# A row-wise log-sum-exp on one core: scalar-engine results in PSUM, more rows for VectorE, logs moved early, a new chunk plan

## The chip, the cores and the metric

One core of a Trainium2 chip. The time is device microseconds of one execution. Every run told here was with a granted clock of 1.0. Five engines run side by side; three matter here. The load queue moves the input from HBM to SBUF, ScalarE (ACT in the profile) computes exponentials and logarithms, and VectorE (DVE) adds up rows. PSUM is the second on-chip memory; in these kernels ScalarE writes results to it and ScalarE and VectorE read them from there.

## The reference

```python
x = np.random.randn(32, 512, 1024).astype(np.float32)
x_max = np.max(x, axis=-1, keepdims=True)
return x_max.squeeze(-1) + np.log(np.sum(np.exp(x - x_max), axis=-1))
```

These are 16,384 rows of 1024 numbers, 128 rows on each of 128 partitions. Both kernels leave the maximum out and compute log(sum(exp(x))).

## The kernel before

The kernel loads the 128 rows of each partition in chunks that become smaller. In a pair such as `(16, 9)`, the first number is the rows of the chunk. The second is how many of them go through ScalarE as one large exponential and are then summed by VectorE. Each of the other rows is one exponential with `accum_out`, which makes ScalarE itself add up the row. The exponentials overwrite the input; only the sums are wanted.

```python
CHUNKS = [
    (12, 4), (14, 4), (16, 4), (16, 9), (16, 11), (12, 8), (10, 6), (8, 5),
    (6, 4), (5, 3), (4, 2), (3, 1), (2, 0), (2, 0), (1, 0),
]
LAST_PARTS = [512, 512]
RING_ROWS = 50
# ... tiles in SBUF: ring [128, 50, 1024], sums [128, 128], part [128, 2], res [128, 128]
    for r, n_dve in CHUNKS:
        # ... slot of the ring
        nc.sync.dma_start(out=ring[:, slot : slot + r], in_=x_v[:, row : row + r])
        if n_dve:
            nc.scalar.activation(out=ring[:, slot : slot + n_dve],
                                 in_=ring[:, slot : slot + n_dve], func=Exp)
            nc.vector.reduce_sum(out=sums[:, row : row + n_dve],
                                 in_=ring[:, slot : slot + n_dve], axis=AX)
        for j in range(n_dve, r):
            nc.scalar.activation(out=ring[:, slot + j], in_=ring[:, slot + j], func=Exp,
                                 accum_out=sums[:, row + j : row + j + 1])
        # ...
    # last row: two loads of 512 columns, each with an accumulating Exp into part[:, k];
    # after the first of them: Ln of all 127 finished rows
    nc.vector.reduce_sum(out=sums[:, row : row + 1], in_=part, axis=AX)
    nc.scalar.activation(out=res[:, row : row + 1], in_=sums[:, row : row + 1], func=Ln)
    nc.scalar.dma_start(out=out_v, in_=res)
```

The softmax here doesn't subtract the row's maximum and nothing guards it: scores larger than these inputs give would overflow.

## Time and profile before

| | before |
|---|---|
| median of the first 3 runs | 166.25 us (166.19 to 166.28) |
| span of the profiled run | 164.9 us |
| last load byte arrives | 159.09 us |
| last half row started on ScalarE | 161.31 us |
| output issued | 162.48 us |

The last load byte comes from the trace's records of single DMA packets; the rows below it are ScalarE's own start times. All are counted from the start of the span.

First the page of before: span, busy time of the engines, the busy tenths of the DMA engines in 40 slices of 4.1 us, and the load queue (packets, MB, share of the time of 16 DMA engines).

```profile
span 164.9 us, 255 instructions
...
DVE 67.1 (41%) x13; ACT 125.7 (76%) x151; POOL 0.2 (0%) x4
...
DMA  6998999997997998999899898999999999999940
...
q1 hardware_dynamic: 2448, 67.11, 95.3%
```

The load queue is busy for 95.3% of the span. The packet records run from 1.74 us to 159.09 us, which is 67.11 MB at 427 GB/s. In the DMA line only the first slice and the last two are low. So about 157 us of the 165 is one unbroken load, and no change of arithmetic shortens it. What can be shortened is the end, after the last byte.

The groups of instructions by form show what one accumulating row costs (busy us, mean ns of one).

```profile
L67 ACT ACTIVATE ring<-ring 128x1024 f32<-128x1024 f32 x66 | 68.7, 1043 | 0.0
...
L67 ACT ACTIVATION_READ_ACCUMULATOR ring<-ring 128x1 f32 x66 | 12.5, 190 | 0.0
```

One row is two instructions, an ACTIVATE of 1043 ns and an ACTIVATION_READ_ACCUMULATOR of 190 ns. They overlap their neighbours, so their sum is not the cost of a row. The cost is the distance from start to start, and that is read from the timeline of ScalarE (start us, length us, what; in brackets the idle time before it and what ended it):

```profile
130.08 4.47 ACT L60 ACTIVATE ring<-ring 128x5120 f32<-128x5120 f32 x1 [0.23 <-DMA ring<-in_x_dram]
...
143.44 2.76 ACT L60 ACTIVATE ring<-ring 128x3072 f32<-128x3072 f32 x1 [0.18 <-DMA ring<-in_x_dram]
...
148.38 1.91 ACT L60 ACTIVATE ring<-ring 128x2048 f32<-128x2048 f32 x1
...
158.42 1.05 ACT L67 ACTIVATE ring<-ring 128x1024 f32<-128x1024 f32 x1
159.36 0.20 ACT L67 ACTIVATION_READ_ACCUMULATOR ring<-ring 128x1 f32 x1
159.46 1.05 ACT L67 ACTIVATE ring<-ring 128x1024 f32<-128x1024 f32 x1
...
161.11 0.31 ACT L92 ACTIVATE res<-sums 128x127 f32<-128x127 f32 x1
161.31 0.63 ACT L84 ACTIVATE ring<-ring 128x512 f32<-128x512 f32 x1
161.82 0.20 ACT L84 ACTIVATION_READ_ACCUMULATOR ring<-ring 128x1 f32 x1
162.25 0.20 ACT L94 ACTIVATE res<-sums 128x1 f32<-128x1 f32 x1 [0.22 <-DVE sums L93]
162.48 0.37 ACTq L95 DMA_DIRECT2D out_dram<-res  x1
```

From 158.42 to 159.46 is 1.04 us: that is one row. The view puts an idle time in brackets only from 0.15 us on. The chunk at 148.38 has none, but the trace has 0.10 us of idle time before it, and its landing is where the chain that ended last (`--critical`) comes in from the loads. From 148.38 until the last Ln ScalarE does not idle, so there it is behind the loads. The last half row could have been started about 0.47 us after the last byte. This is the time at other places between the last packet of a chunk and the exponential that had waited for it: the eight-row chunk's last packet ended at 129.61, and 130.08 is the start. It was started 2.22 us after the last byte, at 161.31. VectorE's timeline at the end:

```profile
153.35 1.22 DVE L63 TENSOR_REDUCE sums<-ring 128x1 f32<-128x1024 f32 x1 [0.74 <-ACT ring L60]
162.06 0.15 DVE L93 TENSOR_REDUCE sums<-part 128x1 f32<-128x2 f32 x1 [7.48 <-ACT ring L84]
```

VectorE had nothing to do for 7.48 us, then added two numbers in 0.15 us, and ScalarE waited 0.22 us for that. From the start of the last half row to the issue of the output is 1.17 us.

### The profile page before, as it was taken

How to read it: one execution, taken by the hardware profiler on the slowest of the kernel's cores; microseconds unless marked ns; L12 is line 12 of the kernel's file. 1: busy time of each engine (PE TensorE's matmuls, PEld its weight loads, DVE VectorE, ACT ScalarE, POOL GpSimd, SP SyncE). 2: the span in 40 equal slices, each digit the busy share in tenths (PEclk: the TensorE clock that was granted, in tenths of full speed). 3: DMA queues.
4: the chain of work that ended last, by engine and by line, in shares of the span. 5: the costliest groups of instructions: out<-in, count | busy, mean ns of one | idle time of the engine just before them, and what ended most of it. 6: DMA issues, size and time to landing. Idle time of an engine off the chain costs nothing.

```text
span 164.9 us, 255 instructions
## 1 busy us (share of the span) xinstructions
DVE 67.1 (41%) x13; ACT 125.7 (76%) x151; POOL 0.2 (0%) x4
## 2 busy tenths in 40 slices
DVE  0000073005400082000099200999996949788300
ACT  3000699249990799919996299999989999999993
POOL 0000000000000000000000000000000000000000
DMA  6998999997997998999899898999999999999940
GB/s 191 477 477 382 445 445 445 445 445 318 509 461 318 493 511 366 397 509 413 350 509 461 358 453 382 421 437 477 389 437 421 427 423 432 426 411 417 415 187 16
DMA packets 2593, 67.18 MB, mean 407 GB/s; under 512 B 288, under 2 KB 416, under 8 KB 800
## 3 DMA queue, kind: packets, MB, share of 16 engines
q1 hardware_dynamic: 2448, 67.11, 95.3%
q10 hardware_dynamic: 144, 0.07, 0.1%
q14 instruction: 1, 0.01, 0.0%
HBM read 67.11 MB, written 0.07 MB: 407 GB/s over the span
## 4 chain that ended last, share of the span: by engine, by line
DMA 54%; ACT 32%; DVE 8%; another core or an unknown queue 3%; issue 1%; SPq 0%; ACTq 0%
DMA ring<-in_x_dram 54%; ACT ring L60 16%; ACT ring L67 15%; DVE sums L63 8%; ACT ring L84 1%; SPq L58 0%; ACT res L94 0%; ACT res L92 0%; DVE sums L93 0%; ACTq L60 0%; ACTq L92 0%
## 5 line engine op out<-in xcount | busy, mean ns | idle before, releaser
L63 DVE TENSOR_REDUCE sums<-ring 128x4 f32<-128x4096 f32 (+8 forms) x12 | 66.9, 5576 | 87.7 <-ACT ring L60 87.7
L60 ACT ACTIVATE ring<-ring 128x4096 f32<-128x4096 f32 (+8 forms) x12 | 54.5, 4539 | 35.8 <-DMA ring<-in_x_dram 35.7
L67 ACT ACTIVATE ring<-ring 128x1024 f32<-128x1024 f32 x66 | 68.7, 1043 | 0.0
L67 ACT ACTIVATION_READ_ACCUMULATOR ring<-ring 128x1 f32 x66 | 12.5, 190 | 0.0
L93 DVE TENSOR_REDUCE sums<-part 128x1 f32<-128x2 f32 x1 | 0.2, 155 | 7.5 <-ACT ring L84 7.5
L52 ACT ACT_TABLE_LOAD x1 | 1.3, 1283 | 0.7 <-PEq L112 0.7
L84 ACT ACTIVATE ring<-ring 128x512 f32<-128x512 f32 x2 | 1.3, 628 | 0.0
L84 ACT ACTIVATION_READ_ACCUMULATOR ring<-ring 128x1 f32 x2 | 0.4, 202 | 0.0
L94 ACT ACTIVATE res<-sums 128x1 f32<-128x1 f32 x1 | 0.2, 203 | 0.2 <-DVE sums L93 0.2
L92 ACT ACTIVATE res<-sums 128x127 f32<-128x127 f32 x1 | 0.3, 308 | 0.0
L112 POOL MEMSET const-bfloat16-1.0<- 128x1 bf16 x1 | 0.1, 102 | 0.0
L112 POOL MEMSET const-uint8-127<- 128x1 uint8 x1 | 0.1, 102 | 0.0
L112 POOL MEMSET const-float32-0.0<- 128x1 f32 x1 | 0.1, 99 | 0.2 <-issue 0.2
L112 POOL MEMSET const-float32-1.0<- 128x1 f32 x1 | 0.1, 99 | 0.0
## 6 DMA issues: line engine op xcount, KB each, us to landing
ring<-in_x_dram SPq DMA_DIRECT2D x2, 6144.0 KB, 27.4
ring<-in_x_dram SPq DMA_DIRECT2D x1, 7168.0 KB, 33.9
ring<-in_x_dram SPq DMA_DIRECT2D x1, 5120.0 KB, 28.3
ring<-in_x_dram SPq DMA_DIRECT2D x1, 4096.0 KB, 14.7
ring<-in_x_dram SPq DMA_DIRECT2D x1, 3072.0 KB, 21.6
ring<-in_x_dram SPq DMA_DIRECT2D x1, 2560.0 KB, 27.3
ring<-in_x_dram SPq DMA_DIRECT2D x1, 2048.0 KB, 24.1
ring<-in_x_dram SPq DMA_DIRECT2D x2, 1024.0 KB, 30.4
```

The lines of the kernel that those rows point to most:

```text
L52: nc.scalar.preload_act_table_set("natural_log_exp_and_others")
L60: nc.scalar.activation(out=ring[:, slot : slot + n_dve], in_=ring[:, slot : slot + n_dve], func=Exp)
L63: nc.vector.reduce_sum(out=sums[:, row : row + n_dve], in_=ring[:, slot : slot + n_dve], axis=AX)
L67: nc.scalar.activation(out=ring[:, slot + j], in_=ring[:, slot + j], func=Exp, accum_out=sums[:, row + j : row + j + 1],)
L84: nc.scalar.activation(out=ring[:, slot, c : c + w], in_=ring[:, slot, c : c + w], func=Exp, accum_out=part[:, k : k + 1],)
L92: nc.scalar.activation(out=res[:, 0:row], in_=sums[:, 0:row], func=Ln)
L93: nc.vector.reduce_sum(out=sums[:, row : row + 1], in_=part, axis=AX)
L94: nc.scalar.activation(out=res[:, row : row + 1], in_=sums[:, row : row + 1], func=Ln)
L112: nc = _bacc.Bacc("TRN2", target_bir_lowering=False, num_devices=1)
```

## The change

The intent was to make ScalarE cheaper at the end: results that nobody reads go to PSUM, and so do most accumulators; more rows of the late chunks go to VectorE; logs of finished rows are taken early; and the last two half sums are joined by Ln itself, as log(1·a + b), without VectorE.

```diff
 CHUNKS = [
-    (12, 4), (14, 4), (16, 4), (16, 9), (16, 11), (12, 8), (10, 6), (8, 5),
-    (6, 4), (5, 3), (4, 2), (3, 1), (2, 0), (2, 0), (1, 0),
+    (10, 4), (16, 6), (16, 6), (16, 10), (15, 10), (13, 8), (11, 7), (8, 5),
+    (6, 4), (5, 4), (3, 2), (3, 2), (2, 1), (1, 0), (1, 0), (1, 0),
 ]
+LN_FROM = 5
 ...
+    apool = ctx.enter_context(tc.tile_pool(name="apool", bufs=4, space=bass.MemoryType.PSUM))
+    jpool = ctx.enter_context(tc.tile_pool(name="jpool", bufs=2, space=bass.MemoryType.PSUM))
 ...
+    def exp_sum(src, w, to):
+        junk = jpool.tile([P, D], fp32, name="junk")
+        nc.scalar.activation(out=junk[:, :w], in_=src, func=Exp, accum_out=to)
 ...
-        for j in range(n_dve, r):
-            nc.scalar.activation(out=ring[:, slot + j], in_=ring[:, slot + j], func=Exp,
-                                 accum_out=sums[:, row + j : row + j + 1])
+        if r - n_dve >= 2:
+            acc = apool.tile([P, r - n_dve], fp32, name="acc")
+            for j in range(n_dve, r):
+                exp_sum(ring[:, s + j], D, acc[:, j - n_dve : j - n_dve + 1])
+            nc.vector.tensor_copy(sums[:, row0 + n_dve : row0 + r], acc)
+        elif r > n_dve:
+            exp_sum(ring[:, s + n_dve], D, sums[:, k : k + 1])
+        if r >= LN_FROM:
+            if row0 > logged:
+                nc.scalar.activation(out=res[:, logged:row0], in_=sums[:, logged:row0], func=Ln)
+                logged = row0
 ...
-    nc.vector.reduce_sum(out=sums[:, row : row + 1], in_=part, axis=AX)
-    nc.scalar.activation(out=res[:, row : row + 1], in_=sums[:, row : row + 1], func=Ln)
+    last = apool.tile([P, 1], fp32, name="acc")
+    exp_sum(ring[:, slot, w0:], w1, last)
+    nc.scalar.activation(out=res[:, row:NB], in_=last, func=Ln, bias=part)
```

(The two forms of the loop are joined over several lines here, and the index `k` is `row0 + n_dve`. The whole diff also turns on `tc.manual_schedule()`. Run e1 below is without it and e2 with it, and their stretches differ by no more than the early Ln, so no effect of it was seen.) There is one thing that the diff doesn't show and the built program does. In a chunk with two or more such rows, every exponential into `acc` except the first waits for the one just before it to complete, because both write the same PSUM tile. There are 42 such waits. In the kernel before there were no such waits: there, two columns of one SBUF tile did not make one row wait for another.

More of the change, by code (lines that the diff above doesn't have):

```diff
@@ L46 @@
     pool = ctx.enter_context(tc.tile_pool(name="pool", bufs=1))
+    apool = ctx.enter_context(tc.tile_pool(name="apool", bufs=4, space=bass.MemoryType.PSUM))
+    jpool = ctx.enter_context(tc.tile_pool(name="jpool", bufs=2, space=bass.MemoryType.PSUM))
     ring = pool.tile([P, RING_ROWS, D], fp32, name="ring")
     sums = pool.tile([P, NB], fp32, name="sums")
-    part = pool.tile([P, len(LAST_PARTS)], fp32, name="part")
+    part = pool.tile([P, 1], fp32, name="part")
     res = pool.tile([P, NB], fp32, name="res")
     nc.scalar.preload_act_table_set("natural_log_exp_and_others")
+    def exp_sum(src, w, to):
+        junk = jpool.tile([P, D], fp32, name="junk")
+        nc.scalar.activation(out=junk[:, :w], in_=src, func=Exp, accum_out=to)
+    ctx.enter_context(tc.manual_schedule())
     row = slot = 0
+    logged = 0
+    w0, w1 = LAST_PARTS
+    plan = []
     for r, n_dve in CHUNKS:
@@ L57 @@
             slot = 0
-        nc.sync.dma_start(out=ring[:, slot : slot + r], in_=x_v[:, row : row + r])
-        if n_dve:
-            nc.scalar.activation(
-                out=ring[:, slot : slot + n_dve], in_=ring[:, slot : slot + n_dve], func=Exp
-            )
-            nc.vector.reduce_sum(
-                out=sums[:, row : row + n_dve], in_=ring[:, slot : slot + n_dve], axis=AX
-            )
-        for j in range(n_dve, r):
-            nc.scalar.activation(
-                out=ring[:, slot + j],
-                in_=ring[:, slot + j],
-                func=Exp,
-                accum_out=sums[:, row + j : row + j + 1],
-            )
+        plan.append((row, slot, r, n_dve))
         slot += r
@@ L77 @@
         slot = 0
-    c = 0
-    for k, w in enumerate(LAST_PARTS):
-        nc.sync.dma_start(out=ring[:, slot, c : c + w], in_=x_v[:, row, c : c + w])
-        c += w
-    c = 0
-    for k, w in enumerate(LAST_PARTS):
-        nc.scalar.activation(
-            out=ring[:, slot, c : c + w],
-            in_=ring[:, slot, c : c + w],
-            func=Exp,
-            accum_out=part[:, k : k + 1],
-        )
-        c += w
-        if k == 0:
-            nc.scalar.activation(out=res[:, 0:row], in_=sums[:, 0:row], func=Ln)
-    nc.vector.reduce_sum(out=sums[:, row : row + 1], in_=part, axis=AX)
-    nc.scalar.activation(out=res[:, row : row + 1], in_=sums[:, row : row + 1], func=Ln)
+    for row0, s, r, n_dve in plan:
+        nc.sync.dma_start(out=ring[:, s : s + r], in_=x_v[:, row0 : row0 + r])
+        if n_dve:
+            nc.scalar.activation(
+                out=ring[:, s : s + n_dve], in_=ring[:, s : s + n_dve], func=Exp
+            )
+            nc.vector.reduce_sum(
+                out=sums[:, row0 : row0 + n_dve], in_=ring[:, s : s + n_dve], axis=AX
+            )
+        if r - n_dve >= 2:
[4 more added lines that the diff above has]
+        elif r > n_dve:
+            k = row0 + n_dve
+            exp_sum(ring[:, s + n_dve], D, sums[:, k : k + 1])
+        if r >= LN_FROM:
+            if row0 > logged:
+                nc.scalar.activation(
+                    out=res[:, logged:row0], in_=sums[:, logged:row0], func=Ln
+                )
+                logged = row0
+    nc.sync.dma_start(out=ring[:, slot, :w0], in_=x_v[:, row, :w0])
+    nc.sync.dma_start(out=ring[:, slot, w0:], in_=x_v[:, row, w0:])
+    exp_sum(ring[:, slot, :w0], w0, part)
+    nc.scalar.activation(out=res[:, logged:row], in_=sums[:, logged:row], func=Ln)
+    last = apool.tile([P, 1], fp32, name="acc")
+    exp_sum(ring[:, slot, w0:], w1, last)
+    nc.scalar.activation(out=res[:, row:NB], in_=last, func=Ln, bias=part)
     nc.scalar.dma_start(out=out_v, in_=res)
```

## The prediction

> **What bounds it now.** The page of before: span 164.9 us, ScalarE 76% busy, VectorE 41%, load queue 95.3% of the DMA engines' time, 67.11 MB read. The packet records run from 1.7 to 159.1 us without a gap: 427 GB/s. So about 157 us is loading, which the change doesn't shorten. Only the tail, 159.1 to 164.9 us, can shrink. The timeline of ScalarE shows it without a real gap from 148.4 us (landing of the four-row chunk) to the last accumulator read at 162.0; landings are seen about 0.47 us after the last packet, so the last half row could have been started at 159.6 and was started at 161.3: ScalarE has about 1.7 us of backlog. Then VectorE's join (0.16), Ln (0.20), hand-overs of 0.04, and 2.4 us of output.
>
> **Costs in the trace.** A row with accumulation repeats every 1.04 us (ACTIVATE 1043 ns plus ACTIVATION_READ_ACCUMULATOR 190 ns, each overlapping its successor by 95 ns). A row in a block costs 0.853 us plus 0.1 per block; VectorE then 1.07 per row.
>
> **What changes.**
> 1. Rows summed by VectorE 61 -> 69: 8 x 0.187 = 1.5 us less on ScalarE, mostly before the tail; in the last 22-23 rows 10 -> 13, about 0.5 us.
> 2. Ten early Ln of 6 to 16 columns, about 0.12 us each, three of them after 138 us: +0.3. The late Ln falls from 308 to about 0.2 us.
> 3. Junk and most accumulators in PSUM. The Trainium skill ("Perfetto Trace Analysis", Optimizing Scalar/DVE Operations) gives ScalarE 93 ns access overhead on SBUF, 51 on PSUM, and says that the profile shows about twice this. Our 190 ns agrees for SBUF; nothing here shows PSUM. I estimate 0 to 45 ns off each instruction, 0 to 80 ns per row.
> 4. A new wait: in the built program each accumulating exponential into a shared accumulator tile, except the first, waits for the one before to complete; its 95 ns overlap is lost and a 40 ns hand-over added. Without PSUM's saving such a row would take 1.17 us, with it about 1.05 to 1.13. Single-row chunks wait only on the row before last: no stall.
> 5. VectorE join removed (0.2 saved); Ln with a bias operand costs about 0.09 more (estimate from "ScalarE: Activation LUTs", What ACT_TABLE_LOAD costs). Net 0.1.
> 6. Smaller last loads: packet times of before (162 ns for 4 KB against 2443 for 64 KB) give +0.1 us of loading. Ring slots still come free 7 us or more before the queue runs dry.
>
> **Sum.** Following ScalarE row by row (for before this gives 161.9; measured 162.0): at 1.04/1.17 us per row it ends at 162.9, at 1.00/1.09 at 161.9, at 0.96/1.05 at 161.2. It cannot be under about 160.5. The accumulator waits hand back most of what the VectorE rows save; only cheaper PSUM writes make it a gain. I take between the last two: 165.8 us, range 164.7 to 167.1. Under 162.9 would need more than the whole backlog.
>
> **What would show it.** Last load byte at about 159.2. Read accumulator to PSUM under 190 ns; start-to-start in groups 1.05 to 1.17; single late rows 0.96 to 1.04. Last half row's start before 161.3 for a gain. VectorE's last reduction near 159, just before the late Ln. Last accumulator read to Ln: one short same-engine wait.
>
> **What would make it wrong.** PSUM writes no cheaper (up to 167) or far cheaper (164.5); the late Ln waiting for VectorE; a changed DMA rate.

## The result

| | before | after |
|---|---|---|
| median, first comparison | 166.26 us (4 runs) | 166.59 us (4 runs, 166.43 to 167.12) |
| ratio after/before, 95% interval | | 1.0025 [1.0002, 1.0048] |
| ratio in a second comparison, on another chip | | 1.0006 [0.9991, 1.0022] |
| span of the profiled run | 164.9 us | 164.9 us |
| last load byte | 159.09 us | 158.88 us |
| last half row started (behind the last byte) | 161.31 (2.22) | 161.35 (2.47) |
| output issued (after that start) | 162.48 (1.17) | 162.31 (0.96) |

A ratio is the mean time of one kernel's fast runs over that of the other's fast runs of the same rounds, so it isn't quite the ratio of the medians quoted. The change does next to nothing to the time. The two comparisons put it at 0.06% and 0.25% slower, and their intervals run from 0.09% faster to 0.48% slower. The page of after has the same shape:

```profile
span 164.9 us, 258 instructions
...
DVE 76.2 (46%) x22; ACT 126.6 (77%) x145; POOL 0.2 (0%) x4
...
DMA  6999997997997998999889999999999999999940
...
q1 hardware_dynamic: 2592, 67.11, 95.2%
```

VectorE has 9 us more work and the load queue is as full as before. The forms of one accumulating row:

```profile
L60 ACT ACTIVATE junk<-ring 128x1024 f32<-128x1024 f32 x58 | 59.3, 1022 | 1.3
...
L60 ACT ACTIVATION_READ_ACCUMULATOR junk<-ring 128x1 f32 x60 | 8.1, 135 | 0.0
```

Each of the two instructions has become shorter: 1043 to 1022 ns, and 190 to 135 ns. A reader who adds these lines up expects rows cheaper by about 75 ns. The timeline shows the opposite:

```profile
121.24 6.18 ACT L80 ACTIVATE ring<-ring 128x7168 f32<-128x7168 f32 x1 [0.70 <-DMA ring<-in_x_dram]
127.32 1.01 ACT L60 ACTIVATE junk<-ring 128x1024 f32<-128x1024 f32 x1
128.26 0.12 ACT L60 ACTIVATION_READ_ACCUMULATOR junk<-ring 128x1 f32 x1
128.42 1.03 ACT L60 ACTIVATE junk<-ring 128x1024 f32<-128x1024 f32 x1
129.38 0.13 ACT L60 ACTIVATION_READ_ACCUMULATOR junk<-ring 128x1 f32 x1
129.54 1.03 ACT L60 ACTIVATE junk<-ring 128x1024 f32<-128x1024 f32 x1
...
131.68 0.20 ACT L97 ACTIVATE res<-sums 128x13 f32<-128x13 f32 x1
131.78 4.46 ACT L80 ACTIVATE ring<-ring 128x5120 f32<-128x5120 f32 x1
...
158.55 1.01 ACT L60 ACTIVATE junk<-ring 128x1024 f32<-128x1024 f32 x1
159.50 0.19 ACT L60 ACTIVATION_READ_ACCUMULATOR junk<-ring 128x1 f32 x1
159.59 1.01 ACT L60 ACTIVATE junk<-ring 128x1024 f32<-128x1024 f32 x1
...
161.24 0.20 ACT L105 ACTIVATE res<-sums 128x16 f32<-128x16 f32 x1
161.35 0.58 ACT L60 ACTIVATE junk<-ring 128x512 f32<-128x512 f32 x1
161.87 0.12 ACT L60 ACTIVATION_READ_ACCUMULATOR junk<-ring 128x1 f32 x1
162.01 0.26 ACT L108 ACTIVATE res<-acc,part 128x1 f32<-128x1 f32 x1
162.31 0.37 ACTq L109 DMA_DIRECT2D out_dram<-res  x1
```

From 127.32 to 128.42 is 1.10 us, and to 129.54 another 1.12. In the trace's nanoseconds the read of the accumulator ends at 128.388 and the next row starts at 128.420. In before the next row started about 0.1 us *before* the read ended (159.46 against 159.36 + 0.20); now it starts 0.03 us after. The early Ln at 131.68 moves the next start by 0.10 us, to 131.78. The single rows at the end (158.55, 159.59) are 1.04 us apart as before. There is no bracket after 121.24, and the trace has no smaller gap over 0.04 us there, so ScalarE has not idled from the landing of the 11-row chunk on. VectorE in the same time:

```profile
148.85 9.93 DVE L83 TENSOR_REDUCE sums<-ring 128x4 f32<-128x4096 f32 x4 [1.24 <-ACT ring L80]
```

This is four reductions in one merged line. It ends at 158.78, well ahead of the late Ln at 161.24, so VectorE does not hold it up.

### The profile page after: what moved, and what is told of

Its sections match the earlier page's. It is cut to its first block, busy times and chain, and to the rows that moved or that the text cites. A ratio compares the mean times of both kernels' runs of the same rounds, so it can differ in the third digit from the quotient of the medians.

```text
span 164.9 us, 258 instructions
## 1 busy us (share of the span) xinstructions
DVE 76.2 (46%) x22; ACT 126.6 (77%) x145; POOL 0.2 (0%) x4
## 3 DMA queue, kind: packets, MB, share of 16 engines
q1 hardware_dynamic: 2592, 67.11, 95.2%
HBM read 67.11 MB, written 0.07 MB: 407 GB/s over the span
## 4 chain that ended last, share of the span: by engine, by line
DMA 54%; ACT 32%; DVE 11%; issue 2%; SPq 0%
DMA ring<-in_x_dram 54%; ACT ring L80 22%; DVE sums L83 11%; ACT junk L60 9%; ACT res L97 0%; SPq L78 0%; ACT res L108 0%; ACT res L105 0%
## 5 line engine op out<-in xcount | busy, mean ns | idle before, releaser
L83 DVE TENSOR_REDUCE sums<-ring 128x4 f32<-128x4096 f32 (+7 forms) x13 | 75.3, 5812 | 71.3 <-ACT ring L80 71.3
L80 ACT ACTIVATE ring<-ring 128x4096 f32<-128x4096 f32 (+7 forms) x13 | 61.4, 4726 | 33.6 <-DMA ring<-in_x_dram 33.6
L60 ACT ACTIVATE junk<-ring 128x1024 f32<-128x1024 f32 (+1 forms) x60 | 60.5, 1008 | 1.3
L60 ACT ACTIVATION_READ_ACCUMULATOR junk<-ring 128x1 f32 x60 | 8.1, 135 | 0.0
L90 DVE COPY sums<-acc 128x6 f32<-128x6 f32 (+5 forms) x9 | 1.4, 158 | 11.2 <-ACT junk L60 11.2
L97 ACT ACTIVATE res<-sums 128x16 f32<-128x16 f32 (+6 forms) x9 | 1.8, 203 | 0.0
```

The lines of the kernel that those rows point to most:

```text
L60: nc.scalar.activation(out=junk[:, :w], in_=src, func=Exp, accum_out=to)
L80: nc.scalar.activation(out=ring[:, s : s + n_dve], in_=ring[:, s : s + n_dve], func=Exp)
L83: nc.vector.reduce_sum(out=sums[:, row0 : row0 + n_dve], in_=ring[:, s : s + n_dve], axis=AX)
L90: nc.vector.tensor_copy(sums[:, row0 + n_dve : row0 + r], acc)
L97: nc.scalar.activation(out=res[:, logged:row0], in_=sums[:, logged:row0], func=Ln)
```

## A measure for the experiments

The loading differs from run to run. In the profiled runs the last byte arrived between 158.75 and 159.31 us, also for one and the same kernel (158.88 and 158.75 for the kernel after). This spread of 0.56 us is as large as most effects here. But the time after the last byte has two parts that hardly vary. The *lag* is from the last byte to the start of the last half row. It was 2.47 and 2.48 us in the two profiles of the kernel after, and 2.22 us in both profiles of kernels with before's plan and rows. The *end part* is from that start to the issue of the output. Where ScalarE no longer waits for loads after the 11-row chunk of the new plan, there is also the *stretch*: from the start of that chunk's large exponential to the start of the last half row, ScalarE's own work without idle time (only e5 has 0.06 us of it). It was 40.11 us in both profiles of the kernel after.

| run | one row to the next in a group, us | stretch, us | lag, us | end part, us | ratio to before, 95% interval |
|---|---|---|---|---|---|
| before | 1.04 | – | 2.22 | 1.17 | 1 |
| after | 1.12 | 40.11 | 2.47 | 0.96 | 1.0025 [1.0002, 1.0048] |
| after_again | 1.12 | 40.11 | 2.48 | 0.96 | 1.0006 [0.9991, 1.0022] |
| e1_plan_only | 1.04 | 39.43 | 1.84 | 1.16 | 0.9990 [0.9978, 1.0003] |
| f2_psum_junk_only | 1.04 | 39.43 | 1.84 | 1.16 | 0.9979 [0.9967, 0.9991] |
| e2_sbuf_acc | 1.04 | 39.74 | 2.13 | 0.96 | 0.9989 [0.9977, 1.0002] |
| f3_one_junk | 1.18 | 41.18 | 3.54 | 0.98 | 1.0083 [1.0069, 1.0096] |
| e3_two_acc | 1.00 | 39.36 | 1.74 | 1.00 | 0.9968 [0.9954, 0.9981] |
| e7_late_two_acc | 1.12, then 1.00 | 39.37 | 1.73 | 0.99 | 0.9966 [0.9948, 0.9983] |
| e4_no_early_ln | 1.12 | 39.81 | 2.21 | 0.96 | 0.9992 [0.9979, 1.0004] |
| e5_two_acc_few_ln | 1.00 | 39.21 | 1.55 | 0.96 | 0.9967 [0.9949, 0.9985] |
| f1_join_only | 1.04 | – | 2.22 | 0.99 | 0.9998 [0.9986, 1.0011] |
| e6_finer_plan | 1.00 | – | 1.19 | 0.97 | 0.9944 [0.9928, 0.9960] |

All of them give the reference's result. Kernels e1 to e4 ran together on one chip, e5 to e7 with after_again on another, f1 to f3 in a third call; each of these was timed in five rounds. The chips differ a little: before itself took 166.53, 166.40 and 166.38 us. The absolute times in the expectations start from the first comparison, so the ratios are what to compare.

## The experiments

My theory was: the new wait on the shared accumulator tile makes a row dearer than it was, and this and the early Ln in ScalarE's busy stretch eat what the plan and the join bring. Rivals: the plan itself costs (A); the early Ln alone cost (B); the PSUM results themselves are what costs or saves (C).

### e1_plan_only: the new plan alone

```diff
 # kernel before
-CHUNKS = [(12, 4), (14, 4), ...]
+CHUNKS = [(10, 4), (16, 6), ...]   # as in after; nothing else
```

> The kernel before with nothing but the new chunk plan (exponentials kept in place, sums in SBUF, one late Ln, join by VectorE). Theory (the plan is good, waits and early Ln on the shared accumulators eat its gain): ScalarE row by row ends 0.35 us earlier than before, so about 165.9 us, ratio to before about 0.998. Rival A (the plan itself is what costs, by more small loads and more VectorE rows in the tail): 166.5 us or more, ratio 1.002 or above, and the late Ln waits for VectorE.

The stretch was 39.43 us, 0.68 less than in the kernel after with the same plan, and the lag 1.84 us, 0.38 less than before's. The median was 166.39 us against 166.53 for before on that chip. Rival A falls by these two spans; the ratio alone, whose interval contains 1, would not decide it. The plan is a small gain, and the rest of the change takes it away again on this stretch. The plan has one more effect: ScalarE's last idle time was before 148.38 in before and is before 121.72 here. So under the new plan all work added to ScalarE after 121 us counts. Under the old one the idle times before 130.08, 143.44 and 148.38 (0.23, 0.18 and 0.10 us) could have taken in a little of it; that is read from the trace and was not tested.

### e2_sbuf_acc: no shared accumulator

```diff
 # kernel after
-        if r - n_dve >= 2:
-            acc = apool.tile(...)      # and the copies by VectorE
-        ...
+        for j in range(n_dve, r):
+            exp_sum(ring[:, s + j], D, sums[:, row0 + j : row0 + j + 1])
```

> The kernel after with every accumulating exponential writing its sum straight to the sums tile in SBUF: no shared PSUM accumulator, no VectorE copies; unused exponentials still in PSUM, early Ln kept. Theory (the wait on the shared accumulator tile costs about 0.08 us a row): start-to-start of rows in groups falls from 1.12 to 1.04 us, the exponentials end about 0.4 us earlier, about 166.2 us against 166.6 for after. Rival C (PSUM junk is what costs or saves): rows not at 1.04. Rival B (the early Ln alone cost): no change from after, 166.6.

Rows are back at 1.04 us and the stretch is 39.74 us, 0.37 less than after. The median was 166.34 us. What is left above e1's 39.43 is 0.31 us; e4 shows the same amount for the early Ln.

### e3_two_acc: the accumulators in PSUM, without the wait

```diff
 # kernel after
-            acc = apool.tile([P, r - n_dve], fp32, name="acc")
+            acc = [apool.tile([P, (m + 1) // 2], fp32, name="acc"),
+                   bpool.tile([P, (m + 1) // 2], fp32, name="accb")]
             for j in range(m):
+                exp_sum(ring[:, s + n_dve + j], D, acc[j % 2][:, j // 2 : j // 2 + 1])
 # and two strided copies to sums; apool and bpool have two buffers each
```

> The kernel after with two PSUM accumulator tiles used in turn, so that a row waits on the row before last only; one more VectorE copy per chunk. Theory (it is the wait, not the place): start-to-start 1.04 us or a little less although accumulators are in PSUM, read accumulator still about 130 ns, total like the SBUF variant, about 166.2 us. Rival (PSUM accumulators are slower in themselves): start-to-start stays near 1.12 us and total 166.6. If PSUM shortened the cycle as well, start-to-start would be 1.00 us or less.

Better than I had expected: 166.04 us, and rows 1.00 us apart.

```profile
127.72 1.01 ACT L61 ACTIVATE junk<-ring 128x1024 f32<-128x1024 f32 x1
128.67 0.12 ACT L61 ACTIVATION_READ_ACCUMULATOR junk<-ring 128x1 f32 x1
128.72 1.02 ACT L61 ACTIVATE junk<-ring 128x1024 f32<-128x1024 f32 x1
129.67 0.13 ACT L61 ACTIVATION_READ_ACCUMULATOR junk<-ring 128x1 f32 x1
129.72 1.03 ACT L61 ACTIVATE junk<-ring 128x1024 f32<-128x1024 f32 x1
```

The next row starts at 128.72, 50 ns after the start of the read at 128.67. In before that distance was 93 ns. So a PSUM accumulator does make a row cheaper, by 0.04 us, and with the wait gone this comes through. (The recorded lengths drift along this trace, between 1.01 and 1.09 us, while the distances stay; I don't know why, and no reading here rests on them.)

### e4_no_early_ln: one late Ln

```diff
-LN_FROM = 5
+LN_FROM = 99
```

> The kernel after without the early Ln: one Ln over 127 columns after the first half row, accumulators in PSUM with their waits kept. Theory: three early Ln of 0.11 us fall in the stretch where ScalarE never idles (from 121 us on) and the late Ln grows by 0.09, so the exponentials end 0.25 to 0.35 us earlier: about 166.3 us. Rival (early Ln are free or help): 166.6 us or more.

The stretch is 39.81 us, 0.30 less than after. Four early Ln of 0.10 us each had stood in it (I had counted three), and the late Ln of 127 columns takes 0.20 us instead of 0.11. Together with e2 the account closes: 40.11 - 0.37 - 0.30 = 39.44, and the plan alone measured 39.43. The median was 166.45 us, within the interval of no difference to before.

### f2_psum_junk_only: unused exponentials in PSUM, nothing else

```diff
 # e1_plan_only
-                out=ring[:, slot + j],
+                out=junk,              # one of two PSUM tiles
```

> The run with the new plan only, and the unused exponentials sent to two PSUM tiles; sums in SBUF, late Ln and VectorE join as before. Theory: where the unused result goes does not change the cycle of a row: ACTIVATE is recorded some 40 ns shorter, but start-to-start stays 1.04 us and ScalarE needs 39.4 us from the landing of the 11-row chunk to the last half row, as with the plan alone. Rival (PSUM writes make rows cheaper): start-to-start 1.00 us, 0.7 us less in that stretch.

```profile
127.32 1.01 ACT L69 ACTIVATE junk<-ring 128x1024 f32<-128x1024 f32 x1
128.27 0.19 ACT L69 ACTIVATION_READ_ACCUMULATOR junk<-ring 128x1 f32 x1
128.36 1.01 ACT L69 ACTIVATE junk<-ring 128x1024 f32<-128x1024 f32 x1
```

The ACTIVATE is recorded 1.01 us long instead of 1.04, but the next row still starts 1.04 us later, and the stretch is 39.43 us as with the plan alone. So this part of the change is worth nothing here. The ratio of 0.9979 against e1's 0.9990 is within both intervals.

### f3_one_junk: the wait without a PSUM accumulator

```diff
 # e2_sbuf_acc
-    jpool = ... name="jpool", bufs=2
+    jpool = ... name="jpool", bufs=1
```

> The SBUF-accumulator variant with one junk tile instead of two, so that each accumulating exponential waits on the one before through the junk tile and no PSUM accumulator has any part in it. Theory (the wait alone costs the lost overlap and the hand-over): start-to-start 1.17 to 1.20 us where rows follow each other; about ten such waits after the 11-row chunk landed, so that stretch grows from 39.7 to about 41.1 us; ratio to before about 1.007. Rival (the 1.12 us of the kernel after came from the PSUM accumulator and not from the wait): still 1.04 us, ratio 0.999.

```profile
127.76 1.01 ACT L60 ACTIVATE junk<-ring 128x1024 f32<-128x1024 f32 x1
128.70 0.19 ACT L60 ACTIVATION_READ_ACCUMULATOR junk<-ring 128x1 f32 x1
128.92 1.03 ACT L60 ACTIVATE junk<-ring 128x1024 f32<-128x1024 f32 x1
```

The accumulator is in SBUF, the read takes its full 0.19 us, and the next row starts 30 ns after its end: 1.16 to 1.18 us from start to start. The stretch grew to 41.18 us and the time to 167.73 us. The wait alone, through another tile and without a PSUM accumulator, costs 0.14 us for each row that has to wait, and the ten waits expected in the stretch make up its growth of 1.44 us. That settles wait against place.

### after_again: the control

> The kernel after, unchanged, as a control beside the other three on the same chip. Expected: ratio to before 1.001 to 1.003, as in its first measurement; rows in groups at 1.12 us, ScalarE without idle time from the landing of the 11-row chunk on.

The stretch and the end part came out to the hundredth as in the first profile; the ratio was 1.0006, a little under the range expected.

### e7_late_two_acc: two tiles in the late chunks only

```diff
 # e3_two_acc
+        two = 2 if row0 >= 86 else 1   # acc[j % two], and so on
```

> Two accumulator tiles in turn only in the chunks from row 86 on (groups of 4, 3 and 2 rows); the five large chunks before keep the shared tile and its waits. Theory (only waits in the stretch where ScalarE never idles count): groups before at 1.12 us a row, after at 1.00; total as with two tiles everywhere, ratio to before about 0.997, 0.5 to 0.8 us under the kernel after. Rival (all waits count, in proportion): of the 42 waiting rows only 6 are relieved, so almost no gain over the kernel after.

The groups before 121 us ran at 1.12 us a row, those after it at 1.00, and the stretch was 39.37 us against 39.36 with two tiles everywhere. Of the 42 waits of the kernel after, 36 cost nothing, because ScalarE waited for the next load afterwards anyway.

### e5_two_acc_few_ln: early Ln only where ScalarE waits anyway

```diff
 # e3_two_acc
-LN_FROM = 5
+LN_FROM = 12
```

> Two accumulator tiles in turn, and early Ln only after chunks of 12 rows or more, that is where ScalarE waits for a load anyway; the late Ln has 54 columns. Theory: four Ln of 0.10 us leave the busy stretch, the late one grows by 0.03, so 0.1 to 0.3 us less than with two tiles alone: ratio to before about 0.9955. Rival (Ln placement doesn't matter): 0.997 as with two tiles alone.

The stretch fell by 0.15 us, less than the four Ln that left it (0.40, minus 0.03 for the longer late one). ScalarE had now caught up with the loads at the five-row chunk (it idled for less than 0.1 us until that chunk landed at 144.44), and so what counts from there on is the work after that landing. In time no difference to e3 was seen: 0.9967 against 0.9968. The expected 0.9955 was a miss.

### f1_join_only: the join by bias

```diff
 # kernel before
-            accum_out=part[:, k : k + 1],
+            accum_out=part[:, 0:1] if k == 0 else last,     # last: [P, 1] in PSUM
-    nc.vector.reduce_sum(out=sums[:, row : row + 1], in_=part, axis=AX)
-    nc.scalar.activation(out=res[:, row : row + 1], in_=sums[:, row : row + 1], func=Ln)
+    nc.scalar.activation(out=res[:, row : row + 1], in_=last, func=Ln, bias=part[:, 0:1])
```

> The kernel before with only the last join changed: second half row accumulates into PSUM, Ln takes the first half's sum as bias, no VectorE reduction. Expected from the two traces: from the start of the last half row to the issue of the output 0.96 us instead of 1.17, so 0.2 us less, ratio to before about 0.9988. My prediction had said 0.1. If the bias operand cost more than it saves, 1.17 or more.

The end part is 0.99 us instead of 1.17, and the lag is unchanged at 2.22. I had expected 0.96 and a ratio of 0.9988. The ratio, 0.9998, is too coarse to show 0.18 us out of 166.

### e6_finer_plan: the best version

```diff
 # e5_two_acc_few_ln
+CHUNKS = [
+    (12, 4), (13, 4), (13, 4), (12, 8), (13, 9), (12, 7), (11, 7), (8, 4), (8, 5),
+    (7, 5), (5, 3), (4, 3), (3, 2), (2, 2), (1, 0), (1, 1), (1, 1), (1, 0),
+]
```

> The last one with a finer chunk plan (no chunk over 13 rows, 18 chunks instead of 16, two of the last single rows summed by VectorE). By row-by-row arithmetic with 1.00 us per PSUM row, ScalarE catches up with the loads near the end: last half row started about 0.5 us earlier than with two tiles alone; ratio to before 0.992 to 0.995, about 165.4 us. Rival (small loads cost more than they bring, or VectorE holds up the late Ln): no better than the run without the finer plan; the last load byte would be seen later than 159.3 us, or the late Ln would wait for VectorE.

```profile
136.11 4.47 ACT L81 ACTIVATE ring<-ring 128x5120 f32<-128x5120 f32 x1 [1.05 <-DMA ring<-in_x_dram]
...
160.05 0.19 ACT L61 ACTIVATION_READ_ACCUMULATOR junk<-ring 128x1 f32 x1
160.24 0.26 ACT L116 ACTIVATE res<-sums 128x64 f32<-128x64 f32 x1
160.40 0.58 ACT L61 ACTIVATE junk<-ring 128x512 f32<-128x512 f32 x1
```

```profile
149.94 10.21 DVE L84 TENSOR_REDUCE sums<-ring 128x3 f32<-128x3072 f32 x5 [0.32 <-ACT ring L81]
```

It took 165.66 us against 166.40 for before on that chip, ratio 0.9944, and against 166.65 for the kernel after. The gain over before is real and small: the lag is 1.19 us. What the finer plan itself adds to e5 is 0.36 us of lag; by the clock it is 165.66 against 165.97 us, with intervals that overlap. ScalarE's last idle time is now at 136.11, so the landing of the seven-row chunk has become the point from which its work counts. VectorE (second fence, five reductions merged) ends at 160.15, and the late Ln starts after it at 160.24, 0.09 us after ScalarE could have started it (in before the Ln starts 0.10 us after the read in front of it does, 161.01 and 161.11). So VectorE has no room left for more rows at the end. The last half row may start 0.47 us after the last byte; at most 0.7 us of lag is left.

## Why the prediction was right, and where its terms were off

**The range held, the centre did not.** I had said 165.8 us with 164.7 to 167.1. Measured: 166.59 and 166.65 us. I expected a small gain and none came. The range held because it was wide enough for a gain of 1% as well as for a loss of half a per cent; that the result lies in it is no proof of the terms. Right was the frame: the loading of 157 us doesn't change, and of the end of about 6 us only some 1.7 us of backlog and the join can go, so a gain of over 2% was out of reach. The queue stayed at 95.2%, and no ring slot held it up.

**The step that was mis-sized is point 3, "I estimate 0 to 45 ns off each instruction, 0 to 80 ns per row", and the choice made from it, "between the last two".** The measured costs are 1.04 us for a single row (not 0.96 to 1.00) and 1.12 for a row in a group (not 1.05 to 1.09). The unused result in PSUM saves nothing from start to start (f2). The accumulator in PSUM saves 0.04 us per row (e3), and only in groups, since single rows keep their sums in SBUF in this kernel. I counted both as savings, and for every row. The prediction had named this case under what would make it wrong ("PSUM writes no cheaper (up to 167)"). My own sum had a line for the case nearest to what came (1.04/1.17, ending at 162.9), and I gave it too little weight. Even this one ends 0.9 us later than the 162.0 that was measured. Six waiting rows at 1.17 us instead of 1.12 make 0.3 of this, and a last byte taken to arrive 0.3 us later than it did another 0.3; the rest is not traced.

**Point 4, the new wait, was right in mechanism and size.** I gave 1.05 to 1.13 us for a waiting row with PSUM's saving; 1.10 to 1.12 were measured. Without PSUM's saving I gave 1.17, and f3 measured 1.16 to 1.18. Against the same row in PSUM without the wait (1.00) it costs 0.12 us, and this turns the 0.04 that PSUM saves into a loss of 0.08. I did not say that only the six waits after 121 us count; e7 shows that.

**Point 2, the early Ln, was right in its total**: I gave +0.3, and e4 measured 0.30 net. Two errors offset each other in it: I had three of about 0.12 us each after 138 us, and the stretch without idle time begins at 121 and holds four of 0.10. They stand where ScalarE has no idle time.

**Point 5, the join, was half of what it is.** "Net 0.1"; 0.21 in the two traces, 0.18 when done alone. The Ln with a bias operand takes 261 ns against 203, so the extra was some 35 ns less than I had taken, though its source is in PSUM now and the two effects are not separated. I had also left out that the last read into PSUM ends earlier: 0.12 against 0.20 us.

**Point 6, loading**: predicted +0.1 us; the last byte arrived 0.2 us earlier, inside the spread of 0.56 us, so this stays undecided.

**Where the expected gain went.** From the last byte to the output, the kernel after gave 0.21 us in the join and took 0.25 in the lag. In the lag, the plan alone gives 0.38 us (2.22 to 1.84); the early Ln take back 0.30 and the waits of groups, PSUM's saving included, 0.37. The sum, +0.29 in the lag, agrees with the measured 0.25 within 0.04. So the traces say no change within 0.05 us. The clock said 0.06% to 0.25% more (0.1 to 0.4 us); one interval contains zero and the other nearly reaches it. Whether there is a real loss of 0.2 us on top of this account is left open; it is smaller than the spread of the loading.

## What to carry to other kernels

Read the cost of a repeated instruction from start to start: here both instructions of a row became shorter in the profile and the row became longer. When results of one engine in a row go to one PSUM tile, look in the built program for a wait on the instruction just before; two tiles used in turn took it away and turned a loss into a gain (1.12 to 1.00 us a row). In a kernel bound by its loads, find the last moment at which the compute engine idles: only work after that moment costs time, so put side work such as early logarithms before it. For the waits e7 shows this in stretch and time; for the logarithms e5 shows it in the stretch (0.15 us) and not in the time.

## What the Trainium skill lacked or had wrong

- "Perfetto Trace Analysis", Optimizing Scalar/DVE Operations, gives ScalarE an access overhead of about 93 ns on SBUF and 51 on PSUM. The runs show where a destination in PSUM brings this difference and where it doesn't. For an ACTIVATE with its source in SBUF and its unused result in PSUM nothing is saved from start to start (1.04 us in e1 and in f2); only its recorded length falls (1043 ns in before, 1005 in f2). That would fit the page's remark that the write-acknowledgement half overlaps the next instruction. For the read of the accumulator the destination decides: the next instruction starts 0.09 to 0.10 us after it with SBUF and 0.05 us with PSUM (f2 and e3), which agrees with the page's two figures.
- "ScalarE: Activation LUTs", Step-by-step: what each stage is for, recommends PSUM as an ACTIVATE's destination, as the lower-latency port. The recorded length agrees; the distance from row to row did not change (f2).
- "VectorE: DVE Perf Modes", The DRAIN you can't avoid, finds that a semaphore after each VectorE instruction costs nothing extra. I found no page with the figure for ScalarE. There a wait on the instruction just before costs 0.12 us with a PSUM accumulator (1.12 against 1.00) and 0.14 with one in SBUF (1.18 against 1.04).
- "DMA: Bandwidth & Descriptors", Where 436 GB/s comes from, says that for transfers between HBM and SBUF the HBM side, at about 358 GB/s, binds. This kernel on one core loaded 67.11 MB in 157.35 us, which is 427 GB/s. The table of measured bandwidths on the same page (425 GB/s for 16 MB) agrees with the run, and the note under it says that its figures are for one core and that about 358 GB/s is what each gets when both cores of an HBM domain load. The sentence about what binds lacks this condition; no run here has a second core loading.
